# Bias adds and two low parts of the feed-forward by accumulating DMA, and the last rows of the down weights loaded in quarters

## The chip, the cores and the metric

The kernel runs on one core of a Trainium2 chip. The metric is the device time of one execution in microseconds, lower is better. The engines are named as in the profile: PE (matmuls) with PEld (its weight loads), DVE (vector engine), ACT (scalar engine), POOL (general engine, which also issues the accumulating DMAs) and SP (which issues the weight loads).

## The reference

Two layers on x of 512 rows by 1024, in fp32. Each layer has two half-step feed-forwards around a mixer (mLSTM in layer 0, gated MLP in layer 1) and ends with a gated embedding (PLE); each residual update is a layer norm with scale g and bias b.

```python
def layer_norm(x, g, b):
    ...
    y = (x32 - mu) * lax.rsqrt(var + LN_EPS) * g.astype(jnp.float32) + b.astype(jnp.float32)
...
def swiglu_ffn(x, w_gu, w_d):
    g, u = jnp.split(x @ w_gu, 2, axis=-1)
    return (jax.nn.silu(g) * u) @ w_d
...
    for i in range(DEPTH):
        x = layer_norm(DN_ALPHA * x + 0.5 * swiglu_ffn(x, ffn1_wgu[i], ffn1_wd[i]), ln_g[i, 0], ln_b[i, 0])
        ...
        x = layer_norm(DN_ALPHA * x + mix, ln_g[i, 1], ln_b[i, 1])
        x = layer_norm(DN_ALPHA * x + 0.5 * swiglu_ffn(x, ffn2_wgu[i], ffn2_wd[i]), ln_g[i, 2], ln_b[i, 2])
        ple = jax.nn.sigmoid(x @ ple_wg[i] + ple_bg[i]) * (p[i] @ ple_wp[i])
        x = layer_norm(DN_ALPHA * x + ple, ln_g[i, 3], ln_b[i, 3])
```

The hidden width of a feed-forward is 2816, 22 blocks of 128.

## The kernel before, in words

**Numbers in two parts.** An fp32 operand is split into a high part (ACT copies it rounded, L275 for weights, L393 elsewhere) and a low part (the operand less the high part). A product is three matmuls: high by high, high by low, low by high (`mm3`, L388 to L390). The low part of a weight is made in one of three ways: DVE subtracts at once (L284); or, in the phase that `W.apart` marks (chunks 2 to 5 of a feed-forward), DVE subtracts late, when the tile is about to be taken (L290, in `done`); or ACT writes the negated source into the low tile (L281) and a DMA that POOL issues adds the source onto it (L282). The program calls the last "by DMA".

**The stages.** Feed-forward (0,0), mLSTM, feed-forward (0,2), PLE, feed-forward (1,0), gated MLP, feed-forward (1,2), PLE. A feed-forward takes its 22 blocks in chunks of 2, 4, 4, 4, 4, 4 (`FFN_CHUNKS`). Chunks 0 and 1 are projected plainly. From chunk 2 on (`UP_FROM`) a pair of blocks is computed in seven products of half the size (`up_forms`, tile `ups`), from sums and differences of quarters of x (`UpForms`: t1 to t4, x's "forms") and of quarters of the weights. Four loads of 512 KB (tiles `wbox`, two to a raw slot) feed one pair. The ways down of chunks 0 to 4 are done beside the next chunk in seven products too (`Group`, tile `gps`, weights `wquarter`). The last chunk's way down is plain: `down` (psum `dps`), over four row tiles t of x, each with four weight rows k; the activations are in tiles that also have the name `wquarter`. It adds the product to x (L763, "residual"), gathers statistics (L726), and norms the row tile (L740, or L744 and L746 when scale and bias are applied at once).

**Deferred scale and bias.** Where the next stage is not PLE's last norm, the norm that ends a stage only subtracts the mean and multiplies by the deviation (L740). g and b go into the copies of x for the matmuls when x is transposed (L636), and x's own rows get them later, one row tile at a time: `finish` (L755 by g, L756 plus b), which `run_affine` calls. In a feed-forward that is once at the end of chunk 0 and after turns 0, 1, 2 of chunk 1. The row's first residual (L761) reads it. The first feed-forward has nothing to finish; the other three have four rows each. The two mixers have four each too.

**Who makes what when.** `Weights` keeps one list of all weight tiles (`W.order`) in the order in which PE takes them, and one of loads. A raw tile needs one of three slots of 8 KB a partition; a box takes half of one. A split tile needs a free place of its kind (`main` four, `rows` two, `rowsx` one). `release` frees a place and calls `fill`, which forms the next tiles of the list as long as there is a place and the raw data have been loaded. In the apart phase one more rule holds (L257): a tile whose load was recorded within the last two products is not formed yet, and nothing behind it is. The order of instructions on every engine follows from where these calls stand; engines run their instructions in that order.

**The end of a feed-forward.** The last chunk has two pairs of blocks, so 14 up products, with the seven down products of chunk 4 between them (releases of kind `rows`), and then `down`. In `W.order` the four rows of wd for `down` come last (`add_rows`, two loads of 1 MB, one for two rows). Behind them stand the first tiles of the next stage: the mLSTM's input weights, the embedding's `ple_wp`, or the gated MLP's input weights. Low parts that are still pending when the 14 products are over are subtracted by `W.lows()` at the end of `up_products`, ahead of `down`'s first residual on DVE.

Of the kernel before, what the change touches and what calls it, by code (L numbers as in the profile page):

```python
# [13 lines left out]
OP = mybir.AluOpType  # L14
# [30 lines left out]
PLE_EXTRA = 3  # L45
UP_BY_DMA = (1, 3, 4, 5, 6)
UP_BY_DMA_2 = (1, 3, 5, 6)


class Weights:  # L50
# [307 lines left out]
def hybrid_trunk(ctx: ExitStack, tc, x, p, ln_g, ln_b, ffn1_wgu, ffn1_wd, ffn2_wgu, ffn2_wd,  # L358
# [33 lines left out]
    def split(hi, lo, src):  # L392
        sca.activation(hi, src, AF.Copy)  # L393
        vec.tensor_sub(lo, src, hi.bitcast(F32))
# [64 lines left out]
    def add_rows(w, kb, n, kind="main"):  # L459
        for k in range(0, n, 2):  # L460
            W.add((kp(w)[:, kb + k:kb + k + 2, :], rows2), kind=kinds_of(kind, k))
# [13 lines left out]
    def ffn_weights(wgu, wd, name, ple=False):  # L475
        starts = [sum(FFN_CHUNKS[:c]) for c in range(LAST + 1)]

        def forms(c):
            m = FFN_CHUNKS[c] // 2

            def quarter(i, j):
                k = starts[c] + m * i
                return kp(wd)[:, k:k + m, j * 512:(j + 1) * 512]
            loads = [W.add_load(quarter(i, j), n, name) for i, j, n in ((0, 0, 2), (0, 1, 1), (1, 1, 1), (1, 0, 2))]
            return W.forms("rows", *((j, slice(None)) for j in loads))

        first = len(W.order)
        for at in range(starts[UP_FROM]):
            if at == 0 or at == starts[UP_FROM] - 1:
                W.add(*((kp(wgu)[:, :, c0:c0 + P], [slice(None)]) for c0 in (at * P, HID + at * P)))  # L490
            elif at % 2:
                add_pairs(wgu, at * P, HID + at * P)
        tiles = W.order[first:]
        del W.order[first:]
        for c, n in enumerate(FFN_CHUNKS):
            down_w = deque(forms(c - 1) if c else ())
            if c >= UP_FROM:
                products = []
                for b in range(starts[c], starts[c] + n, 2):
                    products += W.up_forms(*(W.add_load(kp(wgu)[:, k:k + 4, c0:c0 + 2 * P], 1, "box")  # L500
                                             for c0 in (b * P, HID + b * P) for k in (0, 4)),
                                            by_dma=UP_BY_DMA if b == starts[c] else UP_BY_DMA_2)
                for s, product in enumerate(products):
                    W.order.append(product)
                    if s % 2:
                        W.order.append(down_w.popleft())
                continue
            for i in range(2 * n):
                W.order.append(tiles[2 * starts[c] + i])
                if down_w:  # L510
                    W.order.append(down_w.popleft())
        if ple:
            W.add_hook("rows", lambda hi, lo: turn_p.pop()(hi, lo))
        add_rows(wd, starts[LAST], 4, ["rowsx", "rows", "main", "main"] if ple else ["main", "rows", "rowsx", "rows"])


    ML_SLOTS = (2, 3, 4, 5, 6, 7, 11)
# [191 lines left out]
    class Norm:  # L709
# [41 lines left out]
            self.prepare(t)  # L751
            self.scale(t)

        def finish(self, t):
            vec.tensor_mul(xt[:, t], xt[:, t], self.g_bc)  # L755
            vec.tensor_add(xt[:, t], xt[:, t], self.b_bc)  # L756

    def residual(t, half, ps, first):
        dst = xt[:, t, half * 512:(half + 1) * 512]
# [9 lines left out]
        if hooks:  # L769
            hooks.pop(0)()  # L770

    def run_affine(n=1):
        for _ in range(n):
            if affine:
                affine.pop(0)()

    def set_hooks(norm):
        def turn(t, half):
            return lambda: turn_x(t, halves=(half,), norm=norm)

        def last_turn():
            turn(TB - 1, 1)()
            W.refill(4)

        hooks.extend([turn(TB - 2, 0), turn(TB - 2, 1), turn(TB - 1, 0), last_turn])
        if norm.deferred:
            affine.extend([lambda t=t: norm.finish(t) for t in range(TB)])

    def down(hs, first, norm=None, lazy=False, defer=False):

# [195 lines left out]
    class UpForms:  # L986


        def __init__(self, pool, late):

            f32 = lambda at, tag: at.tile([P, 4, 256], F32, name="x_" + tag, tag=tag)
            a = [tmp.tile([P, 2, 256], F32, name="x_a", tag="pad", bufs=3) for _ in range(2)]
            b, c = f32(pool, "f1"), f32(pool, "f0")
            both = act.tile([P, 2, 4, 256], F32R, name="t1", tag="gb")
            self.t1, self.t2, self.t4 = [both[:, 0], both[:, 1]], [], []
            self.t3 = self.quarter(0, 1)
            whole, halves = slice(0, 4), (slice(0, 2), slice(2, 4))

            def joined(dst, k, t, s=whole):
                vec.tensor_add(dst, *(p[:, s].bitcast(F32) for p in self.quarter(k, t)))  # L1000

            def f32r(to, at, tag):
                to.append(at.tile([P, 4, 256], F32R, name="t_" + tag, tag=tag))
                return to[-1]

            def x22():
                for i, s in enumerate(halves):
                    joined(a[i], 1, 1, s)

            def t3():  # L1010
                for i, s in enumerate(halves):
                    vec.tensor_sub(b[:, s], a[i], b[:, s])

            def t1():
                for i, s in enumerate(halves):
                    vec.tensor_sub(a[i], a[i], c[:, s])

            def split_t1():
                for i, s in enumerate(halves):
                    split(self.t1[0][:, s], self.t1[1][:, s], a[i])  # L1020

            def split_t2():
                split(f32r(self.t2, late, "whi"), f32r(self.t2, late, "wlo"), c)

            self.steps = [
                x22, lambda: joined(b, 0, 1), t3, lambda: joined(c, 0, 0), lambda: vec.tensor_add(c, b, c),
                split_t2, t1, split_t1]

            d = [tmp.tile([P, 2, 256], F32, name="x_d", tag="pad", bufs=3) for _ in range(2)]

            def x21():
                for i, s in enumerate(halves):
                    joined(d[i], 1, 0, s)

            def t4():
                for i, s in enumerate(halves):
                    vec.tensor_sub(d[i], d[i], c[:, s])

            def t4_high():
                hi = f32r(self.t4, pool, "f1")  # L1040
                for i, s in enumerate(halves):
                    sca.activation(hi[:, s], d[i], AF.Copy)

            def t4_low():
                lo = f32r(self.t4, pool, "f0")
                for i, s in enumerate(halves):
                    vec.tensor_sub(lo[:, s], d[i], self.t4[0][:, s].bitcast(F32))

            self.steps += [x21, t4]
            self.last = {0: lambda: split(*self.t3, b), 1: t4_high, 2: t4_low}  # L1050
            self.right = [self.quarter(0, 0), self.quarter(1, 0), self.t2, self.t1, self.t3,
                          self.quarter(1, 1), self.t4]
# [56 lines left out]
    def ffn(layer, k, rows, late, prepare=None):  # L1109
        with stage_pool("forms", 2) as fpool, stage_pool("quarters", Q_BUFS) as qpool, \  # L1110
# [55 lines left out]
            for c, n in enumerate(FFN_CHUNKS):  # L1166
# [13 lines left out]
                for i in range(2 * n if c < UP_FROM else 0):  # L1180
                    b = i // 2
                    ps = project()
                    W.clock += 2
                    if group is not None and i:
                        group.add()
                    if i % 2 == 0:
                        sg = tmp_tile("sg")
                        sca.activation(sg, ps, AF.Silu)
                        W.release()
                    else:  # L1190
                        hf = h[:, b] if c < LAST else tmp_tile("hf")
                        vec.scalar_tensor_tensor(hf, sg, 0.5, ps, op0=OP.mult, op1=OP.mult)
                        if c == LAST:
                            hs.append(halves(W.spare(name)))
                            split(*hs[b], hf)
                        W.release()
                        run_hook()
                    if group is not None and i < 7:
                        group.product()
                        W.release(kind="rows")  # L1200
                        group.form()
                    if c == 1 and i < 3:
                        run_affine()
                    if formed is not None and (i and c == UP_FROM - 2 or i > 0 and c == UP_FROM - 1):
                        formed.step()
                    if c and i == 6:
                        next_group = Group(h, fpool)
                        next_group.form()
# [6 lines left out]
                if c == 0:  # L1215
                    group = Group(h, fpool, c == 0)
                    group.form()
                    group.form()
                if c == 0:
                    run_affine()  # L1220
            W.apart = False
            return down(hs, False, norm, lazy=layer == 0, defer=prepare is not None)

# [726 lines left out]
```

## Time and profile before

| what | value |
|---|---|
| time, median of 3 runs | 2196.89 us (2192.62 to 2197.5) |
| the profiled execution's own time | 2193.39 us |
| its span | 2191.7 us |
| PE busy | 2170.3 us, 99% of the span, 12821 matmuls |
| DVE busy | 1760.5 us, 80% |
| ACT busy | 1208.1 us, 55% |
| POOL busy | 226.3 us, 10% |
| granted TensorE clock | 0.999 |

A row of the timeline gives the start, the duration, the engine, the line and operation, the tiles (out<-in) and shapes, a count, and in brackets how long the engine had been idle and what ended the idle time. Matmuls overlap, so the pitch from one start to the next is what counts for PE; at the full pace it is shorter than a matmul's duration. A row of the groups gives count, busy time in all, mean ns of one, and the idle time ahead.

### The profile page before, as it was taken

Reading aid. Unit: us, or ns where it says so; the run is one execution under the profiler, and the core shown is the slowest. Engines: PE = TensorE matmul, PEld = TensorE weight load, DVE = VectorE, ACT = ScalarE, POOL = GpSimd, SP = SyncE. Lnnn points to the kernel's source line nnn. Section 1 sums busy time; section 2 is a strip of 40 time slices with the busy share of each in tenths; the row PEclk is TensorE's granted clock in tenths of the full one; section 3 lists DMA queues with packets and bytes.
Section 4 is the critical chain, followed back from the end, with each engine's and each line's share of the span. In section 5 each row is a group of like instructions: output and inputs, shape, how many; then the busy total and the mean of one; then the engine's idle time right before and its main releaser. Section 6 shows DMA issues by size and latency. Waiting matters only on the chain.

```text
span 2191.7 us, 32537 instructions
## 1 busy us (share of the span) xinstructions
PE 2170.3 (99%) x12821; PEld 1922.0 (88%) x12821; DVE 1760.5 (80%) x2532; ACT 1208.1 (55%) x1668; POOL 226.3 (10%) x279
## 2 busy tenths in 40 slices
PE   9999999999999999999999999999999999999998
PEld 8899997888888889999888899997888888999987
DVE  5898877786767789888887998877788679988887
ACT  4576656454546445667444566655345553666642
POOL 1011100011101101111000011110001100111100
PEclk9999999999999999999999999999999999999999
DMA  6587764366857426887531587754437743777651
GB/s 187 156 204 184 172 153 136 92 154 128 155 130 154 135 81 163 200 194 172 173 125 58 153 207 186 176 145 135 144 77 140 168 135 116 179 191 179 135 183 58
DMA packets 228097, 329.46 MB, mean 150 GB/s; under 512 B 9140, under 2 KB 163892, under 8 KB 227944
## 3 DMA queue, kind: packets, MB, share of 16 engines
q1 hardware_dynamic: 169104, 211.83, 29.8%
q0 software_dynamic: 52224, 100.86, 27.5%
q10 hardware_dynamic: 6616, 14.69, 1.9%
q8 instruction: 101, 1.65, 0.3%
q14 instruction: 52, 0.43, 0.1%
HBM read 224.58 MB, written 2.11 MB: 103 GB/s over the span
## 4 chain that ended last, share of the span: by engine, by line
PE 78%; DVE 11%; issue 4%; ACT 4%; DMA 3%; SPq 0%; POOL 0%; DVEq 0%; ACTq 0%; POOLq 0%
PE ups L390 7%; PE ups L388 7%; PE ups L389 7%; PE gps L388 6%; PE gps L389 6%; PE gps L390 6%; DMA wlo<-wbox 2%; PE dps L389 2%; PE dps L390 2%; PE dps L388 2%; DVE wlo L290 2%; PE fps L388 2%; PE fps L389 1%; PE fps L390 1%; ACT whi L275 1%
## 5 line engine op out<-in xcount | busy, mean ns | idle before, releaser
L275 ACT ACTIVATE whi<-wbox 128x1024 fp32r<-128x1024 f32 x224 | 235.7, 1054 | 242.2 <-DVE wbox L141 96.9
L390 PE MATMUL ups<-xh,wlo 128*128 128x256 f32 x1024 | 290.3, 284 | 3.2 <-DMA wlo<-wbox 3.2
L388 PE MATMUL ups<-xh,whi 128*128 128x256 f32 x1024 | 289.9, 283 | 0.0
L389 PE MATMUL ups<-xl,whi 128*128 128x256 f32 x1024 | 289.7, 283 | 0.0
L275 ACT ACTIVATE whi<-wraw 128x1024 fp32r<-128x1024 f32 (+1 forms) x212 | 217.3, 1046 | 96.7 <-DVE wraw L119 22.6
L388 PE MATMUL gps<-whi,fhi 128*128 128x512 f32 x644 | 253.0, 393 | 0.4
L389 PE MATMUL gps<-wlo,fhi 128*128 128x512 f32 x644 | 252.2, 392 | 0.0
L390 PE MATMUL gps<-whi,flo 128*128 128x512 f32 x644 | 251.4, 390 | 0.0
L282 POOL DMA_DIRECT2D wlo<-wbox x144 | 122.2, 848 | 1076.8 <-ACT wlo L281 705.0
L763 DVE TENSOR_TENSOR xt<-xt,gps 128x512 f32<-128x512 f32 x302 | 194.9, 680 | 26.7 <-PE gps L390 26.7
L284 DVE TENSOR_TENSOR wlo<-wraw,whi 128x1024 fp32r<-128x1024 f32 (+1 forms) x140 | 167.6, 1214 | 41.8 <-ACT whi L275 40.9
L390 PEld LDWEIGHTS ups<-xh,wlo 128*128 128x128 f32 x1024 | 196.2, 192 | 4.3 <-DMA wlo<-wbox 4.2
L388 PEld LDWEIGHTS ups<-xh,whi 128*128 128x128 f32 x1024 | 196.1, 192 | 3.8 <-ACT us L1085 1.6
L389 PEld LDWEIGHTS ups<-xl,whi 128*128 128x128 f32 x1024 | 196.1, 192 | 2.3
L275 ACT ACTIVATE whi<-wquarter 128x1024 fp32r<-128x1024 f32 (+1 forms) x140 | 135.3, 966 | 77.0 <-DVE wquarter L119 28.9
L281 ACT ACTIVATE wlo<-wbox 128x1024 fp32r<-128x1024 f32 x144 | 150.4, 1044 | 0.0
L390 PEld LDWEIGHTS gps<-whi,flo 128*128 128x128 f32 x644 | 120.9, 188 | 26.9
L388 PEld LDWEIGHTS gps<-whi,fhi 128*128 128x128 f32 x644 | 121.3, 188 | 23.9 <-issue 1.6
L389 PEld LDWEIGHTS gps<-wlo,fhi 128*128 128x128 f32 x644 | 121.3, 188 | 21.6
L944 DVE TENSOR_TENSOR flo<-h,fhi 128x512 fp32r<-128x512 f32 (+1 forms) x140 | 88.5, 635 | 57.6 <-ACT fhi L941 57.0
L290 DVE TENSOR_TENSOR wlo<-wquarter,whi 128x1024 fp32r<-128x1024 f32 x104 | 126.6, 1218 | 0.0
L388 PE MATMUL fps<-xh,whi 128*128 128x512 f32 x288 | 112.2, 390 | 0.0
(365 smaller groups left out, 5822.4 us busy)
## 6 DMA issues: line engine op xcount, KB each, us to landing
wlo<-wbox POOLq DMA_DIRECT2D x144, 512.0 KB, 5.8
wbox<-in_ffn_wgu_dram SPq DMA_DIRECT2D x128, 512.0 KB, 4.9
wquarter<-in_ffn_wd_dram SPq DMA_DIRECT2D x64, 512.0 KB, 5.8
wraw<-in_ml_w_in_dram SPq DMA_DIRECT2D x24, 1024.0 KB, 5.8
wlo<-wraw POOLq DMA_DIRECT2D x48, 512.0 KB, 6.4
wraw<-in_ffn_wgu_dram SPq DMA_DIRECT2D x15, 1024.0 KB, 6.0
wraw<-in_gm_w_in_dram SPq DMA_DIRECT2D x15, 1024.0 KB, 5.6
wraw<-in_ffn_wgu_dram SPq DMA_DIRECT2D x17, 512.0 KB, 4.8
```

What stands on the lines that cost most here:

```text
L275: self.nc.scalar.activation(hi[:, s], src[:, s], AF.Copy)
L281: self.nc.scalar.activation(lo[:, s], src[:, s], AF.Copy, scale=-1.0)
L282: self.nc.gpsimd.dma_start(lo[:, s], src[:, s], accum_op=OP.add)
L284: self.nc.vector.tensor_sub(lo[:, s], src[:, s], hi[:, s].bitcast(F32))
L290: self.nc.vector.tensor_sub(lo, src, hi.bitcast(F32))
L388: mm(ps, st[0], mv[0], start=start, stop=False, skip_group_check=more)
L389: mm(ps, st[0], mv[1], start=False, stop=False, skip_group_check=more)
L390: mm(ps, st[1], mv[0], start=False, stop=stop, skip_group_check=more)
L763: vec.tensor_add(dst, dst, ps)
L944: vec.tensor_sub(lo, src, hi.bitcast(F32))
```

## The change

Four edits, all in the feed-forward:

1. `run_affine` runs earlier (after turns 1 and 2 of chunk 0 and 0 and 1 of chunk 1), and there the bias is added to the row by an accumulating DMA of 512 KB that POOL issues; L755's multiplication stays on DVE. The mixers call it as before, with DVE.
2. The low parts of the forms t1 and t2 of x are made by a negated copy on ACT and an accumulating DMA; the DVE subtractions go. t1's tile is allocated when it is split, and t2 is split after t1.
3. In the last chunk's second pair of blocks, the fifth of the by-DMA tiles' numbers goes: `UP_BY_DMA_LAST` is (1, 3, 6), so tile 5 gets its low part by DVE.
4. The last four rows of wd load as four boxes of 512 KB, each one recorded with one tile, in place of two loads of 1 MB; before a PLE stage the kinds are in another order.

```diff
+UP_BY_DMA_LAST = (1, 3, 6)
...
-                                            by_dma=UP_BY_DMA if b == starts[c] else UP_BY_DMA_2)
+                                            by_dma=UP_BY_DMA if b == starts[c] else UP_BY_DMA_2 if c < LAST else UP_BY_DMA_LAST)
...
-        add_rows(wd, starts[LAST], 4, ["rowsx", "rows", "main", "main"] if ple else ["main", "rows", "rowsx", "rows"])
+        for k, kind in enumerate(["rowsx", "main", "rows", "main"] if ple else ["main", "rows", "rowsx", "rows"]):
+            at = starts[LAST] + k
+            j = W.add_load(kp(wd)[:, at:at + 1, :], 1, "box")
+            W.order.append((kind, (j,), lambda j=j: (W.raws[j], (j,))))
...
-        def finish(self, t):
+        def finish(self, t, by_dma=False):
             vec.tensor_mul(xt[:, t], xt[:, t], self.g_bc)
-            vec.tensor_add(xt[:, t], xt[:, t], self.b_bc)
+            if by_dma:
+                pool.dma_start(xt[:, t], self.b_bc, accum_op=OP.add)
+            else:
+                vec.tensor_add(xt[:, t], xt[:, t], self.b_bc)
...
-            both = act.tile([P, 2, 4, 256], F32R, name="t1", tag="gb")
-            self.t1, self.t2, self.t4 = [both[:, 0], both[:, 1]], [], []
+            self.t1, self.t2, self.t4 = [], [], []
...
+            def split_by_dma(hi, lo, src):
+                sca.activation(hi, src, AF.Copy)
+                sca.activation(lo, src, AF.Copy, scale=-1.0)
+                nc.gpsimd.dma_start(lo, src, accum_op=OP.add)
...
-                    split(self.t1[0][:, s], self.t1[1][:, s], a[i])
+                    split_by_dma(self.t1[0][:, s], self.t1[1][:, s], a[i])
...
-                split(f32r(self.t2, late, "whi"), f32r(self.t2, late, "wlo"), c)
+                split_by_dma(f32r(self.t2, late, "whi"), f32r(self.t2, late, "wlo"), c)
...
-                split_t2, t1, split_t1]
+                t1, split_t1, split_t2]
...
-                    if c == 1 and i < 3:
-                        run_affine()
+                    if (c, i) in ((0, 1), (0, 2), (1, 0), (1, 1)):
+                        run_affine(by_dma=True)
...
-                if c == 0:
-                    run_affine()
```

PE's own instructions and their order stay the same. Line numbers move: L275, L284, L290 become L276, L285, L291, and L740, L756, L763 become L744, L763, L770.

**DVE between the end of feed-forward (0,0) and the mLSTM.** The rows are those behind the last two residuals of `down`; `wlo<-wraw` are the low parts of the mLSTM's first input weights and `xl` the low part of transposed x. Before:

```order
L730 BN_AGGR mv<-st 128x2
L732 TENSOR_SCALAR rs<-mv 128x1
L740 TENSOR_SCALAR xt<-xt,mv,rs 128x1024
L640 TENSOR_TENSOR xl<-xf,xh 128x4x128 x2
L284 TENSOR_TENSOR wlo<-wraw,whi 128x1024 x4
L640 TENSOR_TENSOR xl<-xf,xh 128x4x128 x2
```

And now:

```order
L734 BN_AGGR mv<-st 128x2
L736 TENSOR_SCALAR rs<-mv 128x1
L744 TENSOR_SCALAR xt<-xt,mv,rs 128x1024
L285 TENSOR_TENSOR wlo<-wraw,whi 128x1024 x6
L644 TENSOR_TENSOR xl<-xf,xh 128x4x128 x4
```

Two more weight tiles are formed here, six in place of four, and all of them stand behind the norm of the last row tile. Before, the first two had been formed in the last chunk: the quarters of wd now hold the half slots longer, the mLSTM's first raw load is recorded later (after 2046 matmuls in place of 1986), and the rule on two products (L257) puts its tiles off until after `down`.

**DVE at the end of the last chunk of feed-forward (0,0).** The rows run from the down product ahead of the last two up sums (L1088, L1104, then the splits of the activations, L394) to the first residual of `down`. Before:

```order
L290 TENSOR_TENSOR wlo<-wraw,whi 128x1024 x2
L1104 SCALAR_TENSOR_TENSOR us<-us 128x512
L394 TENSOR_TENSOR wquarter<-us,wquarter 128x2x256
L1104 SCALAR_TENSOR_TENSOR us<-us,ups 128x512
L394 TENSOR_TENSOR wquarter<-us,wquarter 128x2x256
L763 TENSOR_TENSOR xt<-xt,gps 128x512 x2
L290 TENSOR_TENSOR wlo<-wraw,whi 128x1024 x3
L763 TENSOR_TENSOR xt<-xt,dps 128x512
```

And now:

```order
L291 TENSOR_TENSOR wlo<-wbox,whi 128x1024 x2
L1117 SCALAR_TENSOR_TENSOR us<-us 128x512
L395 TENSOR_TENSOR wquarter<-us,wquarter 128x2x256
L1117 SCALAR_TENSOR_TENSOR us<-us,ups 128x512
L395 TENSOR_TENSOR wquarter<-us,wquarter 128x2x256
L770 TENSOR_TENSOR xt<-xt,gps 128x512 x2
L291 TENSOR_TENSOR wlo<-wbox,whi 128x1024
L770 TENSOR_TENSOR xt<-xt,dps 128x512
```

Three subtractions stood ahead of the first residual of `down`, and one stands there now: the rows of wd come earlier, and the two tiles of the mLSTM are gone from here.

**DVE in `down` of feed-forward (0,2), ahead of PLE.** The rows are those from the norm of the third row tile (L744 and L746, scale and bias at once) to the first residual of the fourth; `wlo<-wraw` are the low parts of `ple_wp`. Before:

```order
L640 TENSOR_TENSOR xl<-xps,xh 128x4x128 x2
L744 SCALAR_TENSOR_TENSOR xt<-xt,mv,gb 128x512 x2
L746 SCALAR_TENSOR_TENSOR xt<-xt,rs,gb 128x512 x2
L284 TENSOR_TENSOR wlo<-wraw,whi 128x1024 x2
L763 TENSOR_TENSOR xt<-xt,dps 128x512
```

And now:

```order
L644 TENSOR_TENSOR xl<-xps,xh 128x4x128 x2
L748 SCALAR_TENSOR_TENSOR xt<-xt,mv,gb 128x512 x2
L750 SCALAR_TENSOR_TENSOR xt<-xt,rs,gb 128x512 x2
L285 TENSOR_TENSOR wlo<-wraw,whi 128x1024 x4
L770 TENSOR_TENSOR xt<-xt,dps 128x512
```

Four tiles of `ple_wp` stand here in place of two. The other two were among five subtractions (L290) ahead of `down`'s first residual before; two stand there now.

More of the change, by code (lines that the diff above doesn't have):

```diff
@@ L770, in run_hook, with run_affine @@
             hooks.pop(0)()
-    def run_affine(n=1):
+    def run_affine(n=1, by_dma=False):
         for _ in range(n):
             if affine:
-                affine.pop(0)()
+                affine.pop(0)(by_dma)
     def set_hooks(norm):
@@ L786, in set_hooks @@
         if norm.deferred:
-            affine.extend([lambda t=t: norm.finish(t) for t in range(TB)])
+            affine.extend([lambda by_dma, t=t: norm.finish(t, by_dma) for t in range(TB)])
     def down(hs, first, norm=None, lazy=False, defer=False):
@@ L1016, in t1 @@
                     vec.tensor_sub(a[i], a[i], c[:, s])
+            def split_by_dma(hi, lo, src):
+                sca.activation(hi, src, AF.Copy)
+                sca.activation(lo, src, AF.Copy, scale=-1.0)
+                nc.gpsimd.dma_start(lo, src, accum_op=OP.add)
             def split_t1():
+                both = act.tile([P, 2, 4, 256], F32R, name="t1", tag="gb")
+                self.t1.extend((both[:, 0], both[:, 1]))
                 for i, s in enumerate(halves):
-                    split(self.t1[0][:, s], self.t1[1][:, s], a[i])
+                    split_by_dma(self.t1[0][:, s], self.t1[1][:, s], a[i])
             def split_t2():
-                split(f32r(self.t2, late, "whi"), f32r(self.t2, late, "wlo"), c)
+                split_by_dma(f32r(self.t2, late, "whi"), f32r(self.t2, late, "wlo"), c)
             self.steps = [
                 x22, lambda: joined(b, 0, 1), t3, lambda: joined(c, 0, 0), lambda: vec.tensor_add(c, b, c),
-                split_t2, t1, split_t1]
+                t1, split_t1, split_t2]
             d = [tmp.tile([P, 2, 256], F32, name="x_d", tag="pad", bufs=3) for _ in range(2)]
```

## The prediction

> **What bounds the kernel.** I read the page first, then PE's waits, then the timeline where those waits stand.
>
> ```profile
> span 2191.7 us, 32537 instructions
> PE 2170.3 (99%) x12821; PEld 1922.0 (88%) x12821; DVE 1760.5 (80%) x2532; ACT 1208.1 (55%) x1668; POOL 226.3 (10%) x279
> ...
> PE dps L389 <- DVE wlo L290: 4.8, 4, 1.6
> PE ups L390 <- DMA wlo<-wbox: 3.9, 6, 1.0
> ```
>
> PE sets the time: it idles for some 21 us of the span, and since its matmuls stay the same in number and order, the change can only move those idle times. DVE, 80% busy, is not the bound: work taken from it counts only where PE waits for it. Two waits come from the parts that the change touches. At the start of each `down` PE waits for a subtracted low part of wd (4.8 us, 4 times), and in `ups` for an accumulating DMA (3.9 us, 6 times). In feed-forward (0,0) they look so:
>
> ```profile
> 318.03 0.28 PE L389 MATMUL ups<-xl,whi 128*128 128x256 f32 x1
> 319.35 0.39 PE L390 MATMUL ups<-xh,wlo 128*128 128x256 f32 x1 [1.04 <-DMA wlo<-wbox]
> 319.57 0.28 PE L388 MATMUL ups<-xh,whi 128*128 128x256 f32 x1
> 319.69 0.28 PE L389 MATMUL ups<-xl,whi 128*128 128x256 f32 x1
> ...
> 326.32 1.23 DVE L290 TENSOR_TENSOR wlo<-wraw,whi 128x1024 fp32r<-128x1024 f32 x1 [2.21 <-ACT whi L275]
> ...
> 333.92 0.50 PE L389 MATMUL dps<-wlo,wquarter 128*128 128x512 f32 x1 [1.60 <-DVE wlo L290]
> ```
>
> The pitch into the wait is 1.32 us and out of it 0.22, against 0.12 at full pace: a wait costs its idle time and about 0.26 us more. I add that below. The 326.32 row shows why `down` waits: DVE itself sat 2.21 us for rows of wd that came late.
>
> **Edits 3 and 4: what goes.** The last pair's tile 5 gets its low part from a 1.22 us subtraction in place of copy and DMA, and the rows of wd are asked for earlier. The other three feed-forwards:
>
> ```profile
> 1071.74 0.39 PE L390 MATMUL ups<-xh,wlo 128*128 128x256 f32 x1 [1.00 <-DMA wlo<-wbox]
> 1080.10 0.39 PE L388 MATMUL dps<-whi,wquarter 128*128 128x512 f32 x1
> 1082.86 0.50 PE L389 MATMUL dps<-wlo,wquarter 128*128 128x512 f32 x1 [0.89 <-DVE wlo L290]
> 1472.09 0.38 PE L390 MATMUL ups<-xh,wlo 128*128 128x256 f32 x1 [0.64 <-DMA wlo<-wbox]
> 1486.37 0.50 PE L389 MATMUL dps<-wlo,wquarter 128*128 128x512 f32 x1 [1.46 <-DVE wlo L290]
> 2103.95 0.50 PE L389 MATMUL dps<-wlo,wquarter 128*128 128x512 f32 x1 [0.89 <-DVE wlo L290]
> ```
>
> The DMA waits go whole: 1.30 + 1.26 + 0.90 = 3.46. At `down` of (0,0) and (1,0) the low parts ahead of the first residual shrink from three to one, so the last one is 2 x 1.22 = 2.4 us sooner than a wait of 1.86 and 1.72 needs: both go, 3.58. Before PLE, in (0,2) and (1,2), one more subtraction stands in the chain ahead of `down` (1.2 us); the first tile's low is then ready in time, but the second's ends about 1084.0, where PE, unhindered, wants it near 1083.3. Of the 1.15 in each, 0.5 is gained: 1.0 in both. Sum of the gains here: 8.0.
>
> **Edit 4: what comes.** The quarters of wd hold the half slots, and the next stage's first tiles are formed after `down`'s last work instead of in the last chunk. At the mLSTM's start the first low part now stands behind the last norm:
>
> ```profile
> 353.97 0.28 PE L866 MATMUL sup<-xh,wlo 128*128 128x256 f32 x1
> ...
> 357.70 0.81 DVE L740 TENSOR_SCALAR xt<-xt,mv,rs 128x1024 f32<-128x1024 f32 x1 [0.66 <-POOL rs L733]
> 359.63 1.22 DVE L284 TENSOR_TENSOR wlo<-wraw,whi 128x1024 fp32r<-128x1024 f32 x1
> ...
> 364.47 0.39 PE L866 MATMUL sup<-xh,whi 128*128 128x256 f32 x1 [0.24 <-ACT xh L639]
> 366.52 0.39 PE L866 MATMUL sup<-xh,whi 128*128 128x256 f32 x1 [0.84 <-ACT xh L639]
> ```
>
> L740 ends at 358.51, a low part takes 1.22, so it is there at 359.65 (starts follow an end by some -0.08): PE, which wants it at 353.97, stands 5.7 us. The later waits that the same stand swallows are 0.24 and 0.84 with 0.26 each, and one of 0.2 for a low part in between: about 1.9. Net +3.8. The six subtractions then end near 365.7 and the four `xl` near 368.2, ahead of PE, which wants the first at 363.83 + 5.7.
>
> Before PLE the first low part of `ple_wp` stands behind three rounds of residual and norm:
>
> ```profile
> 1081.59 5.76 DVE L290 TENSOR_TENSOR wlo<-wraw,whi 128x1024 fp32r<-128x1024 f32 x5
> 1087.26 0.68 DVE L763 TENSOR_TENSOR xt<-xt,dps 128x512 f32<-128x512 f32 x1
> 1092.98 0.68 DVE L763 TENSOR_TENSOR xt<-xt,dps 128x512 f32<-128x512 f32 x1
> 1099.90 0.68 DVE L763 TENSOR_TENSOR xt<-xt,dps 128x512 f32<-128x512 f32 x1
> 1106.82 1.22 DVE L284 TENSOR_TENSOR wlo<-wraw,whi 128x1024 fp32r<-128x1024 f32 x1
> ...
> 1105.23 0.39 PE L389 MATMUL pwp<-wlo,whi 128*128 128x512 f32 x1
> ```
>
> Rounds last 5.72, 6.92 and 6.92. With two subtractions ahead of the first residual in place of five, that residual waits for PE instead: 24 matmuls of 0.23 after 1080.10, with the 0.7 that stays, about 1086.2. Then 19.6 of rounds and 1.2: 1107.0, or up to 0.6 sooner if the first half is added early. PE wants it at 1105.23 - 0.5 = 1104.7. That is 1.7 to 2.3; I take 2.1, with 0.2 for the second tile behind it, 2.3 at each PLE, 4.6. At the gated MLP the first tile's high part is now the one that ACT makes after the last transposes:
>
> ```profile
> 1506.67 2.36 DVE L284 TENSOR_TENSOR wlo<-wraw,whi 128x1024 fp32r<-128x1024 f32 x2 [0.26 <-ACT whi L275]
> 1506.08 0.39 PE L389 MATMUL gvps<-wlo,xh 128*128 128x512 f32 x1
> ```
>
> Low part at 1506.67 + 1.22 = 1507.9, wanted at 1506.08: 1.8. Sum of the losses 3.8 + 4.6 + 1.8 = 10.2. These stands weren't in the trace of before, so their bounds: nothing (if the tiles are ready all the same) to 5.7 + 2 x 2.7 + 2.3 = 13.4 (nothing swallowed, 0.4 to 0.5 more at the last three).
>
> **Edits 1 and 2.** DVE loses these, and ACT and POOL gain others:
>
> ```profile
> L756 DVE TENSOR_TENSOR xt<-xt,gb 128x1024 f32<-128x1024 f32 x20 | 24.5, 1225 | 0.7
> L281 ACT ACTIVATE wlo<-wbox 128x1024 fp32r<-128x1024 f32 x144 | 150.4, 1044 | 0.0
> L282 POOL DMA_DIRECT2D wlo<-wbox x144 | 122.2, 848 | 1076.8 <-ACT wlo L281 705.0 <-DVE wlo L290 85.0 <-DVE h L928 70.9
> 817.81 0.39 PE L390 MATMUL fps<-xh,wlo 128*128 128x512 f32 x1
> 818.34 0.47 PE L388 MATMUL gps<-whi,fhi 128*128 128x512 f32 x1
> ```
>
> Twelve of the 20 bias adds go (14.7 us of DVE) and per feed-forward about two x 1.2 of subtractions; ACT, 55% busy, copies 2.1 more each, POOL issues up to seven more DMAs at 0.85. PE waits for none of this except at 818.34 and its two likes, where the pitch is 0.53 in place of 0.23 and a residual and a bias add precede what it waits for: 0.3 each, 0.9 in all, which I count as gained (0 to 0.9).
>
> Sum: -8.0 - 0.9 + 10.2 = +1.3. The bounds of the parts are -8.9 + 0 and -8.0 + 13.4. The profiled execution took 2193.39, 1.7 above its span and 3.5 below the median of 2196.89. It would become 2194.7, and the median 2198.2. This is below 0.2% (4.4 us), about what a measurement of this kernel can tell from no change: no change.
>
> **The rivals.** *A, the boundaries don't hold PE* (faster). If the next stage's first tiles are ready when PE comes, only the gains stay: 2196.9 - 8.9 = 2188.0. For it speaks that the loads themselves land early; against, the order of DVE, which is fixed: nothing lets a subtraction pass L740 or the norm of the third row tile. 0.16.
>
> *B, the accumulating DMAs come late* (slower). DVE's residual L761 reads the row that now takes its bias from a DMA, and x's forms are read by DVE soon after t1 is made; all DVE work queues behind such a wait, the splits that PE takes included.
>
> ```profile
> wlo<-wbox POOLq DMA_DIRECT2D x144, 512.0 KB, 5.8
> DMA to landing us min/median/max: 4.5/6.0/13.7
> 782.85 1.22 DVE L1000 TENSOR_TENSOR x_f<-xh,xl 128x1024 f32<-128x1024 f32 x1
> 799.37 1.27 DVE L761 SCALAR_TENSOR_TENSOR xt<-xt,gps 128x512 f32<-128x512 f32 x2
> 808.15 1.22 DVE L1000 TENSOR_TENSOR x_f<-xh,xl 128x1024 f32<-128x1024 f32 x1
> 822.51 1.28 DVE L761 SCALAR_TENSOR_TENSOR xt<-xt,gps 128x512 f32<-128x512 f32 x2
> ```
>
> The second row's multiplication now stands just ahead of the first of these `x_f`, the fourth's ahead of the other, so the DMAs have 799.37 - 782.85 = 16.5 and 822.51 - 808.15 = 14.4 us. A DMA lands 5.8 us after its issue, 13.7 at the most. It decides from about 14 us. At 16 or more DVE would stand some 2 us at two of the rows in each of three feed-forwards, and PE after it half of that or all: 3 x 2 to 3 x 4 = 6 to 12 on top of the forecast, 2204 to 2210. [...] 0.13.
>
> *C, the stands at the boundaries are longer than I have them, or the waits at `down` don't go* (slower): 13.4 of losses with 4.4 of gains (the DMA waits and 0.9) is +9.0, 2205.9. It needs the low part of the fourth wd row later than 19 matmuls, 4.3 us, after `down` starts. By the rows of (0,2) two residuals (1.28) and one subtraction (1.2) put it at 2.8, the splits of the activations at up to 3.9. 0.11.
>
> **How the numbers follow.** My forecast has 0.60, its own range 2193 to 2202 (a boundary or a gain off by 4 to 5). Slower by over 0.2% are B, C, less what of them falls short, and a little of the forecast's top: 0.22. Faster: A and a little of the bottom: 0.17. Same 0.61. The range that holds 8 in 10 takes half of A and of B: 2189 to 2204.
>
> **What would show it.** In the profile after, `ups` L390 should wait for DMA about 1.2 us in place of 3.9 (less 1.04, 1.00 and 0.64), and `dps` L389 for DVE's L291 about 0.9 in place of 4.8 (0.7 less 0.26, twice). New waits should stand at `sup` (5.7 once), `pwp` (about 2, twice) and `gvps` (1.8). DVE's busy time should fall by some 25 us with the span unmoved. I am wrong if DVE waits for `xt` from a DMA, if PE's new waits aren't there, or if they add up to over 14.

## The result

| | before | after |
|---|---|---|
| median | 2194.20 us (16 runs, 2192.22 to 2197.5) | 2198.68 us (16 runs, 2195.56 to 2201.99) |
| ratio | | 1.002, 95% interval 1.0012 to 1.0027 |
| profiled execution, its span | 2193.39, 2191.7 us | 2201.99, 2200.2 us |
| granted clock, mean | 0.999 | 0.996 |

The change costs 4.5 us by the medians: as large as what the forecast called no change, and clear of zero. The range held it (2189 to 2204; forecast 2198.2), but over a before of 2196.89, the median of the three runs shown then; against 2194.2 the sum should have read 2195.5, and the change is 3 us dearer than that. The two profiled executions lie 8.5 us apart. Some of that is chance: the profiled one is the slowest of the sixteen of after. Their times spread over 6.4 us, and their mean clock goes from 0.996 (2196.0 to 2200.2 us of span) to 0.998 (2193.8, the shortest).

PE's waits after, engine and line, what it waited for, total, times, longest:

```profile
PE sup L873 <- DVE wlo L285: 5.4, 2, 5.1
PE pwp L390 <- DVE wlo L285: 3.6, 2, 1.8
PE ups L391 <- DMA wlo<-wbox: 2.1, 6, 0.6
PE dps L390 <- DVE wlo L291: 1.6, 2, 0.8
...
PE gvps L390 <- DVE wlo L285: 0.8, 1, 0.8
PE gvps L389 <- ACT whi L276: 0.7, 1, 0.7
```

The two waits of before have shrunk from 4.8 and 3.9 to 1.6 and 2.1, and at each start of a next stage stands the wait that the forecast named: 5.1 at `sup`, 1.8 twice at `pwp`, 1.5 at `gvps`. The waits sum to only some 4 us more than before, though, and the span to 8.5. The rest is in the clock. PE around the mLSTM's start, after (start, duration, instruction, wait ahead of it):

```profile
351.62 0.39 PE L873 MATMUL sup<-xh,whi 128*128 128x256 f32 x1 [0.23 <-ACT whi L276]
357.08 0.58 PE L873 MATMUL sup<-xh,wlo 128*128 128x256 f32 x1 [5.07 <-DVE wlo L285]
357.46 0.41 PE L873 MATMUL sup<-xh,whi 128*128 128x256 f32 x1
357.67 0.41 PE L873 MATMUL sup<-xh,wlo 128*128 128x256 f32 x1
357.88 0.41 PE L873 MATMUL sup<-xh,whi 128*128 128x256 f32 x1
```

And DVE there:

```profile
355.08 0.81 DVE L744 TENSOR_SCALAR xt<-xt,mv,rs 128x1024 f32<-128x1024 f32 x1 [0.66 <-POOL rs L737]
355.81 2.35 DVE L285 TENSOR_TENSOR wlo<-wraw,whi 128x1024 fp32r<-128x1024 f32 x2
```

The low part follows the norm of the last row tile, as the order said. What the order can't say is the pitch behind the wait: 0.21 us in place of 0.12. The stretches right behind the three longest stands (stretch, its length, PE busy, granted clock, DMA share, GB/s):

```profile
357.00:360.00 3.00, 2.92 (x13) 0.50 0.24 32
1109.00:1112.00 3.00, 3.00 (x8) 0.55 0.38 63
2133.00:2136.00 3.00, 2.91 (x7) 0.55 0.25 23
```

PE runs at half clock there. How long can be read from stretches of 1 us at both ends of each half-clock time:

```profile
354.00:355.00 1.00, 0.00 (x0) 0.98 0.00 0
361.00:362.00 1.00, 1.00 (x7) 0.61 1.04 397
1109.00:1110.00 1.00, 1.00 (x4) 0.65 0.00 0
1112.00:1113.00 1.00, 1.00 (x4) 0.64 1.05 410
2133.00:2134.00 1.00, 0.91 (x3) 0.65 0.00 0
2136.00:2137.00 1.00, 1.00 (x4) 0.64 0.95 346
```

An estimate from them takes 1.00 and 0.50, the values of whole stretches here, as the only two: a clock of 0.65 over 1 us is then half clock for 0.70 of it, so the second time runs from 1109.30 to 1112.72. The others run from 354.96 to 361.78 and from 2133.30 to 2136.72. The first begins while PE still stands and lasts 4.7 us behind the stand; the other two last 3.4.

PE's instructions are the same in both kernels, so their starts can be set against each other one by one, and every change of the difference has a place:

| place | forecast | profiled executions |
|---|---|---|
| DMA waits in the last pair's `ups` | -3.5 | -3.7 |
| start of `down`, (0,0) and (1,0) | -3.6 | -3.8 |
| start of `down`, (0,2) and (1,2) | -1.0 | -0.4 (twice -1.27 + 1.06) |
| three pitches at `gps` | -0.9 | -1.2 |
| start of the mLSTM | +3.8 | +6.4 (8.0, less 1.6 of old waits) |
| start of PLE, twice | +4.6 | +7.6 (3.91 and 3.70) |
| start of the gated MLP | +1.8 | +2.0 |
| DMA waits in `ups` of chunk 2 | 0 | about +1.6 |
| sum | +1.3 | +8.5 |

The row on chunk 2 is five small waits of both signs (-0.5 to +1.0) at DMAs that the change doesn't touch; one execution of each kernel stands behind them, and I draw nothing from them.

### The profile page after: what moved, and what is told of

Its sections match the earlier page's. It is cut to its first block, busy times and chain, and to the rows that moved or that the text cites. A ratio compares the mean times of both kernels' runs of the same rounds, so it can differ in the third digit from the quotient of the medians.

```text
span 2200.2 us, 32591 instructions
## 1 busy us (share of the span) xinstructions
PE 2175.4 (99%) x12821; PEld 1926.9 (88%) x12821; DVE 1742.1 (79%) x2512; ACT 1211.3 (55%) x1676; POOL 243.6 (11%) x299
## 3 DMA queue, kind: packets, MB, share of 16 engines
HBM read 224.58 MB, written 2.11 MB: 103 GB/s over the span
## 5 line engine op out<-in xcount | busy, mean ns | idle before, releaser
L276 ACT ACTIVATE whi<-wbox 128x1024 fp32r<-128x1024 f32 x240 | 252.0, 1054 | 242.5 <-DVE wbox L142 87.2
L276 ACT ACTIVATE whi<-wraw 128x1024 fp32r<-128x1024 f32 (+1 forms) x196 | 200.6, 1045 | 79.3 <-DVE wraw L120 22.6
L770 DVE TENSOR_TENSOR xt<-xt,gps 128x512 f32<-128x512 f32 x302 | 195.0, 680 | 27.3 <-PE gps L391 27.3
L285 DVE TENSOR_TENSOR wlo<-wraw,whi 128x1024 fp32r<-128x1024 f32 (+1 forms) x148 | 176.7, 1214 | 40.7 <-ACT whi L276 39.9
L276 ACT ACTIVATE whi<-wquarter 128x1024 fp32r<-128x1024 f32 (+1 forms) x140 | 135.4, 967 | 78.4 <-DVE wquarter L120 25.1
L291 DVE TENSOR_TENSOR wlo<-wquarter,whi 128x1024 fp32r<-128x1024 f32 x104 | 126.7, 1218 | 0.0
```

Of the source, the lines that this page charges most:

```text
L276: self.nc.scalar.activation(hi[:, s], src[:, s], AF.Copy)
L285: self.nc.vector.tensor_sub(lo[:, s], src[:, s], hi[:, s].bitcast(F32))
L291: self.nc.vector.tensor_sub(lo, src, hi.bitcast(F32))
L770: vec.tensor_add(dst, dst, ps)
```

## The experiments

The theory: the loss stands at the first tiles of the next stages, which edit 4 puts off behind `down`, and in the half clock that such a stand brings; edits 1 and 2 cost nothing. The rivals: the added accumulating DMAs carry the loss; the next stage's tiles are held by their loads; the clock falls for another reason. Each run's ratio is to runs of the kernel before on the same chip.

**e1_raw_rows: edit 4 undone.**

```diff
-        for k, kind in enumerate(["rowsx", "main", "rows", "main"] if ple else ["main", "rows", "rowsx", "rows"]):
-            at = starts[LAST] + k
-            j = W.add_load(kp(wd)[:, at:at + 1, :], 1, "box")
-            W.order.append((kind, (j,), lambda j=j: (W.raws[j], (j,))))
+        add_rows(wd, starts[LAST], 4, ["rowsx", "rows", "main", "main"] if ple else ["main", "rows", "rowsx", "rows"])
```

> Edits 1 to 3 alone, the rows of wd by two loads of 1 MB again. Theory (the loss stands at the next stage's first tiles, which edit 4 puts off, and in the half clock behind those stands): the boundaries are as before, the DMA waits in ups go (1.30 + 1.27 + 0.91 + 0.25) and three of 0.39 at gps, the waits at the start of down stay: -4.9 us, 2189.3, ratio 0.9978. Rival (the added accumulating DMAs carry the loss): the loss stays without edit 4, 2196 or more.

Measured: 2188.06, ratio 0.9974 (0.9964 to 0.9983). The boundaries are those of before, and the loss is gone: edit 4 carries it. Two details were not as expected. The DMA wait of the last pair moves one tile on in (0,0), and so, with 0.25 and 0.97, in (0,2) and (1,0), and the waits at `down` of (0,0) and (1,0) go without edit 4:

```profile
322.34 0.39 PE L391 MATMUL ups<-t_f,wlo 128*128 128x256 f32 x1 [1.85 <-DMA wlo<-wbox]
```

Its waits:

```profile
PE ups L391 <- DMA wlo<-wbox: 3.6, 5, 1.9
PE dps L390 <- DVE wlo L291: 1.5, 2, 0.8
```

The second go because SP asks for the last two rows of wd sooner (the loads' time on SP's queue). Before, and then with edit 3:

```profile
310.59 9.21 SPq L239 DMA_DIRECT2D wraw<-in_ffn_wd_dram  x2
```

```profile
309.89 2.59 SPq L240 DMA_DIRECT2D wraw<-in_ffn_wd_dram  x2
```

The two issues lay 9.21 us apart from the first's start to the second's end, and lie 2.59 apart now. Why edit 3 brings them together is argued, not shown: a tile that takes its low part by DMA keeps its box until the DMA has read it (5.8 us from issue to landing, by the median before), and a subtraction by DVE, 1.22 us long, would give the raw slot back earlier. So edit 3 is enough for the waits at `down` of (0,0) and (1,0), which the forecast gave to edit 4's earlier rows; e6 below shows that edit 4 removes them without edit 3 too. And edit 3 without edit 4 only moves three of the DMA waits, which the forecast took to go whole.

**e2_adds_only: edits 1 and 2 alone** (the row above, and `UP_BY_DMA_LAST` with the 5 again).

```diff
-UP_BY_DMA_LAST = (1, 3, 6)
+UP_BY_DMA_LAST = (1, 3, 5, 6)
```

> Edits 1 and 2 alone. Theory: only the three pitches of 0.39 at gps go, -1.2 us, 2193.0, ratio 0.9995; DVE busy about 18 us less. Rival (accumulating DMAs come late or delay the others on POOL): DVE waits for xt or the forms of x from a DMA, ups waits more for low parts, +2 us or more.

Measured: 2193.11 by its median, ratio 0.9999 (0.9991 to 1.0008). The three pitches at `gps` go (-0.39 each); whether the time falls by the 1.2 can't be told within the interval. In the changed kernel DVE never waits for an accumulated row or form; its only waits for a DMA are two for `wlo<-wbox`, 0.5 us together. The landings there of the rows' DMAs, and of t1's and t2's:

```profile
DMA to landing us min/median/max: 4.5/4.7/6.2
```

```profile
DMA to landing us min/median/max: 5.9/7.1/8.1
```

Both are far from the 14 us from which rival B decides.

**e3_fill: the next stage's first tiles formed ahead of `down`.**

```diff
             W.apart = False
+            W.fill()
             return down(hs, False, norm, lazy=layer == 0, defer=prepare is not None)
```

Two or three tiles are now formed there: at the end of feed-forward (0,0) three subtractions (L285) stand ahead of `down`'s first residual on DVE and three in place of six behind the last norm.

> The changed kernel with one more call of fill between the last up product and down, which lets the next stage's first tiles be formed there. Theory: the stands at sup, pwp and gvps go, the gains stay: 9.0 us below the kernel before, 2185.2, ratio 0.996, granted clock 0.999. Rival (these tiles are held by their loads, asked for later, and not by the order of DVE): the stands stay or move to ACT's high part, 2195 or more. Second rival (the subtractions moved ahead of down's first residual hold down): waits of 1 us and more at dps, 2189.

Measured: 2181.23, ratio 0.9943 (0.993 to 0.9957), 13.4 us below the kernel before. All stands at `sup`, `pwp` and `gvps` are gone, the clock is 0.999:

```profile
PE dps L390 <- DVE wlo L291: 1.6, 2, 0.8
...
PE ups L391 <- DMA wlo<-wbox: 0.9, 3, 0.5
PE sup L873 <- DVE wlo L285: 0.3, 1, 0.3
PE sup L873 <- ACT whi L276: 0.2, 1, 0.2
```

The tiles' loads were there; only the order held them. The two waits left at `dps` are those before PLE that the changed kernel has as well. The moved subtractions end at 333.59, where the first residual starts (333.50), and PE waits for nothing in that `down`:

```profile
328.96 1.22 DVE L291 TENSOR_TENSOR wlo<-wbox,whi 128x1024 fp32r<-128x1024 f32 x1
330.10 3.49 DVE L285 TENSOR_TENSOR wlo<-wraw,whi 128x1024 fp32r<-128x1024 f32 x3
333.50 0.68 DVE L770 TENSOR_TENSOR xt<-xt,dps 128x512 f32<-128x512 f32 x1
```

It is 4 us better than expected. 1.6 of that are the old waits at the mLSTM's `sup` for ACT and DVE (1.29 and 0.29), which I had expected back; that they stay away I put down to three tiles, not two, being formed early. The rest is within what the medians and single executions differ by: the profiled execution of this kernel lies 11.3 below that of before.

**e4_busy: the changed kernel, PE kept busy in the stands.** The added products go to banks that the next product overwrites.

```diff
+                for _ in range(busy.pop() if busy else 0):
+                    mm(banks[2][:, :256], w[0][:, 0], xh[:, 0, 0:256], start=True, stop=True)
             low_last(w, ps, 0, 256)
...
                         ps = up_bank("pwp")
+                        for _ in range(0 if t or half else 9):
+                            mm(ps, ph[:, 0, 0:P], ws[0][0][:, 0, 0:512], start=True, stop=True)
```

with `busy = [40]`, so that the first loop runs at the mLSTM alone.

> The changed kernel with matmuls on data already there, overwritten afterwards, that fill the stands: 40 of 256 columns ahead of the mLSTM's first product (4.8 us) and 9 of 512 ahead of each PLE (2.0 us). Theory (PE's standing lowers its clock): the stands end at the same times, but behind them the granted clock is 1.00 in place of 0.5 and the pitch 0.12 and 0.23 in place of 0.21 and 0.43: 2.5 + 2 x 1.7 = 5.9 us under the changed kernel's profiled 2202, 2196, and some 2194 in the median. Rival (the clock falls for another reason, such as the loads that start there): 0.5 there all the same, 2199.

Measured: 2194.88, ratio 1.0004 (0.9995 to 1.0013). The low part comes when it came before, and PE, which has 40 + 2 x 9 = 58 matmuls more to do, is done sooner. The timeline at the mLSTM:

```profile
351.61 5.04 PE L890 MATMUL sup<-xh,whi 128*128 128x256 f32 x40 [0.23 <-ACT whi L276]
356.49 0.28 PE L875 MATMUL sup<-xh,whi 128*128 128x256 f32 x1
357.07 0.38 PE L875 MATMUL sup<-xh,wlo 128*128 128x256 f32 x1 [0.30 <-DVE wlo L285]
357.30 0.28 PE L875 MATMUL sup<-xh,whi 128*128 128x256 f32 x1
357.41 0.28 PE L875 MATMUL sup<-xh,wlo 128*128 128x256 f32 x1
```

And the stretches behind the first two stands:

```profile
357.00:360.00 3.00, 2.93 (x25) 1.00 0.21 27
1106.00:1109.00 3.00, 2.82 (x12) 1.00 0.26 18
```

The wait ends at 357.07 as it did at 357.08, the clock behind it is 1.00 and not 0.50, and 25 matmuls fit into the same 3 us in which 13 did. So the stand itself lowers the clock; the loads that start there (365 GB/s at 362 to 366 in both) don't, and the drop at 354.96 came with no DMA at work. The medians differ by 3.8 us, the spans of the profiled executions by 6.1: what the half clock cost lies between them.

**e7_part_busy and e8_part_busy: how long a stand does it.** As e4, with 25 and 3 matmuls, and with 32 and 5.

```diff
-    busy = [40]
+    busy = [25]
...
-                        for _ in range(0 if t or half else 9):
+                        for _ in range(0 if t or half else 3):
```

> The changed kernel with fewer matmuls in the stands: 25 at the mLSTM, which leaves about 2.2 us idle, 3 at each PLE, which leaves about 1.1. Theory (a stand of about 1.8 us or more halves the clock for some 4 us, a shorter one does not): granted clock 0.5 behind the mLSTM's stand and 1.00 behind those at PLE. [...]

> As before with 32 and 5 matmuls: about 1.3 us idle at the mLSTM and 0.7 at each PLE. Theory: granted clock 1.00 behind all three. Rival (any stand does it): 0.5 behind one of them.

Measured, one execution each, 2196.52 and 2194.79. In the first, PE stood 2.11 us at the mLSTM and 1.11 at PLE:

```profile
355.94 0.38 PE L875 MATMUL sup<-xh,wlo 128*128 128x256 f32 x1 [2.11 <-DVE wlo L285]
356.17 0.28 PE L875 MATMUL sup<-xh,whi 128*128 128x256 f32 x1
...
356.67 0.42 PE L875 MATMUL sup<-xh,whi 128*128 128x256 f32 x1
356.88 0.42 PE L875 MATMUL sup<-xh,wlo 128*128 128x256 f32 x1
...
1106.23 0.50 PE L390 MATMUL pwp<-wlo,whi 128*128 128x512 f32 x1 [1.11 <-DVE wlo L285]
```

The stretch behind the second:

```profile
1106.00:1109.00 3.00, 2.60 (x10) 1.00 0.26 22
```

Half clock after the first, though four matmuls late (the pitch goes from 0.12 to 0.21, and the clock is 0.57 over 356 to 360), and full clock after the second. (At the other PLE PE stood 1.12 and kept the full clock too, 1.00 over 2128.5 to 2131.) In the other kernel 1.27 us at the mLSTM were not enough, as the timeline and the stretch behind show:

```profile
356.04 0.38 PE L875 MATMUL sup<-xh,wlo 128*128 128x256 f32 x1 [1.27 <-DVE wlo L285]
```

```profile
355.00:360.00 5.00, 3.96 (x33) 1.00 0.31 92
```

At these four stands the theory holds. The bound isn't sharp: see the last section.

**e5_fill_no_adds and e6_fill_no_edit3: what each part is worth beside the call of `fill`.** The first is the kernel before with edits 3 and 4 and `W.fill()`; the second is e3_fill with tile 5 by DMA again (`UP_BY_DMA_LAST = (1, 3, 5, 6)`).

> Edits 3 and 4 with the call of fill, without edits 1 and 2 (DVE adds the biases and subtracts the forms' low parts). Theory (edits 1 and 2 are worth three pitches of 0.39): 1.2 us above e3_fill, 2182.4, ratio 0.995. Rival (DVE's 18 us matter wherever DVE is behind): +4 us or more, 2185.

> Edits 1, 2 and 4 with the call of fill, tile 5 of the last pair by copy and DMA again. Theory (edit 3 removes the DMA waits of the last pair): 1.30 + 1.27 + 0.91 + 0.25 come back, 3.7 us above e3_fill, 2185. Rival (edit 4's earlier loads alone make these waits go): no change from e3_fill, 2181.

Measured: 2183.17, ratio 0.9946 (0.9934 to 0.9959), and 2183.16, ratio 0.9947 (0.9933 to 0.996). Without edits 1 and 2 it is 1.9 us above e3_fill by the medians, 1.5 when each is taken against the kernel before on its own chip, and 1.7 in the profiled executions, of which three pitches of 0.39 are seen at their places; that is nearer to the theory's 1.2 than to the rival's 4. Without edit 3 it is the same 1.9 and 1.5, but 0.7 in the profiled executions, and the waits come back by 0.4 only:

```profile
PE dps L390 <- DVE wlo L291: 1.6, 2, 0.8
...
PE ups L391 <- DMA wlo<-wbox: 1.3, 4, 0.5
```

That is nearer to the rival: where edit 4 brings the rows of wd early, the DMA waits of the last pair are gone with or without edit 3, and so are the waits at `down` of (0,0) and (1,0): the two left at `dps` are those before PLE. Why earlier rows of wd also end those waits was not traced further. Both pairs of intervals overlap, so the size of each share, a microsecond or two, is not settled.

## Why the prediction was right, and where it was off

- **PE sets the time, and only its waits move.** Right: its 12821 matmuls kept their order, and DVE's busy time fell by 18 us (forecast 25, which left out edit 3's four subtractions, 4.9) without any gain from that but the three pitches of 0.39.
- **The gains at `ups` and `down`.** Right in place and nearly in size (-8.0 forecast, -7.9 measured), but not by the edits named: the `down` waits of (0,0) and (1,0) go with edit 3 alone (e1) and without it (e6, with `fill`), and the `ups` waits go with edit 4, while edit 3 alone only moves three of them one tile on. Before PLE less was gained, 0.2 in place of 0.5 each: the wait for the second row was 0.79 with 0.27 around it.
- **The stands at the boundaries.** Right in place and in length: 5.07 and 0.23 idle for 5.7, 1.79 for 1.7 to 2.3, 0.67 and 0.76 for 1.8. The step that failed is the price of a stand, "a wait costs its idle time and about 0.26 us more". That rule was read off waits of up to 1.6 us. Behind stands of 5.1 and twice 1.8 the clock was halved for 4.7 and twice 3.4 us, and the matmuls there cost 2.2, 1.9 and 1.7 us more: 5.8 in this profiled execution, which is most of the 7.2 by which the two differ from the sum. e4 shows it by removing it.
- **Rival A** fell: the boundaries do hold PE. e3 shows what it would have been, had the order not held the tiles.
- **Rival B** fell: twelve such DMAs, issued into a DVE that is 79% busy, landed 4.5 to 6.2 us after their issue and made nobody wait.
- **Rival C** was right in its first half only so far as the boundaries cost more than forecast; the stands themselves weren't longer, and it didn't name the clock. The waits at `down` did go.
- **The base.** The forecast was made over the median of three runs, 2196.89; over sixteen it is 2194.2. That offset of 2.7 us and the 3 us by which the change is dearer nearly cancel in the time, not in the difference: that the time came within 0.5 us of the forecast is luck.

## What to carry to other kernels

When loads are asked for in another size or order, look at who comes next in the same slots: an earlier load here was a later one there, and a rule that puts off one tile puts off all behind it. A stand of PE has to be priced with the clock behind it: at PLE 1.79 us of waiting, twice, cost another 1.7 to 1.9. Before rebuilding, ask whether the data are there and only the order holds them: one call at the right place turned +4.5 us into -13.4.

## What the runs showed of the hardware

The stand that halves PE's clock has no sharp length here. PE stood 1.60 us at `down` both in the kernel before and in e2, as the waits and the stretches behind show. Before:

```profile
333.92 0.50 PE L389 MATMUL dps<-wlo,wquarter 128*128 128x512 f32 x1 [1.60 <-DVE wlo L290]
```

```profile
333.00:337.00 4.00, 3.08 (x13) 1.00 0.48 147
```

And e2:

```profile
1486.20 0.76 PE L390 MATMUL dps<-wlo,wquarter 128*128 128x512 f32 x1 [1.60 <-DVE wlo L291]
```

```profile
1486.00:1489.00 3.00, 2.80 (x7) 0.54 0.53 133
```

The same wait left the clock at 1.00 once and halved it once. 1.79 halved it twice (0.55 over 1109 to 1112 and over 2133 to 2136 in the kernel after), 2.11 did in e7 (0.57 over 356 to 360) and 5.07 in the kernel after (0.50 over 357 to 360). 1.46 in the kernel before didn't (1.00 over 1485 to 1488), nor did 1.27 in e8, nor 1.11 and 1.12 in e7 (1.00 behind each). For the 1.85 of e1 there is only the mean clock of its execution, 0.999 as in the kernel before, against 0.998 in e2: it speaks against a halving. In the kernel after half clock lasted 3.42 us at each PLE and 6.82 at the mLSTM, by the estimate in the section on the result; the drops came 2.95 us after the stand at the mLSTM began and 2.41 and 2.00 after those at PLE, so not at a fixed time. What decides whether a stand halves the clock stays open. That waits of one length do it at one place and not at another may be why sixteen runs of after spread over 6.4 us, as many of before, with waits of 1.6, over 5.3, and the five of e3, which has no wait above 0.8 behind its start, over 1.4; this is not shown run by run.
